# A two-layer hybrid encoder: the SSD gates as channel tiles among the heads, low parts of the odd weights by DMA

## The chip, the cores and the metric

The kernel runs on one core of a Trainium2 chip. The metric is the device time of one execution in microseconds; where several runs are shown, their median.

## The reference

The network has two layers on x of 512 positions and 1024 channels, and a final RMSNorm. The even layer (latent attention and a Conformer convolution) is not touched here. The odd layer, which the change is about, is:

```python
def odd_layer(x, norm_g, w_in, ...):
    u = rms_norm(x, norm_g) @ w_in                    # 1024 -> 1536 + 2560 + 48 + 4 x 512
    z_c, xbc, dt_f, dt_b, g_b, g_c, h_d, z_d = jnp.split(u, ...)
    o_c = ssd_mixer(z_c, xbc, dt_f, dt_b, ...)        # bidirectional Mamba-2
    o_d = short_conv(g_b, g_c, h_d, conv_d_w) * jax.nn.silu(z_d)
    return x + concatenate([o_c, o_d]) @ w_out        # 2048 -> 1024

def ssd_mixer(...):
    xbc = silu(dw_conv(xbc, conv_w) + conv_b)         # width 5, over positions
    xs, bm, cm = ...                                  # 24 heads of 64; B and C: 4 groups of 128
    y = ssd_scan(forward) + flip(ssd_scan(backward)) + d_skip * xs
    y = y * silu(z)                                   # the gate, 1536 channels
    return rms_norm(y in 4 groups of 384) * norm_g
```

`ssd_scan` works in 4 chunks of 128 positions: inside a chunk (C B^T, weighted by decays) times X; between chunks a state of 128 x 64 a head, carried with decays. All is float32.

## The kernel before

**Products in three parts.** Each float32 matmul operand is split into a high part (rounded to fp32r) and a low part (the rest), and a product is hi.hi + lo.hi + hi.lo: three fp32r matmuls. Activations are split once a layer (`xT`). Weights are split as they come, by the class `Weights`: `_prepare` takes the next slab of a list that has the order of use, loads it (an SP DMA) into `w_raw` (2 buffers), copies it with rounding to `w_hi` on ACT (line 87), and subtracts on DVE or POOL to get `w_lo` (line 88; 3 buffers each). For the odd layer's input projection the subtraction is POOL's. `next` hands out a slab and prepares up to `ahead + 1` = 2 slabs.

**Tiles of the odd layer's input projection.** `odd_tiles` lists the order. A *channel tile* (`mm_cm`, line 318) computes 128 channels x 512 positions in one PSUM bank `acc` (3 banks): 24 matmuls of 512 columns. A *token tile* product (`mm_tm`, line 345) has positions on the partitions. The gates z are made as token tiles, group by group (384 channels; in group 0 also the 48 raw dt columns): 4 position tiles, each 24 matmuls. They come first, all four groups of them, then the channel tiles: C, B and three x tiles of a group, and four short-convolution pieces (h, gc, gb, zd).

`channel_tile` also does what follows the product. For C, B and x: `conv5`, one ACT pass (line 718), four DVE taps that read PSUM (line 720), and a SiLU on ACT and DVE (lines 721 and 722). B and x are then transposed by PE into bank `sb` (line 266) and copied by ACT (lines 748 and 754), in the same call. `fill(n)` works off the next n entries of the list.

**SSD.** While group 1's gates run on PE, a chain on DVE, ACT and PE makes the step sizes dt and their running sums (lines 784 to 827). Then, for each of the 4 groups:

- `ssd_prepare`: C.B products (line 849), two masked copies, the chunk states (line 862 on PE, with DVE 860 and 868, POOL 867, ACT 865), one direction after the other.
- `ssd_pairs`, three pairs of heads: for each head the factor matrix f (ACT 898 and 903, DVE 899 and 904 in 128-column pieces, then Exp, line 906, and the product, line 907), its matmuls with x (line 910, bank `cv`), then the sums with the off-diagonal part (PE 926, DVE 919, 931, 934), the gate multiply on POOL (line 936), and `fill` with 1 to 3 channel tiles.
- `ssd_finish`: the group's RMSNorm (ACT 946, DVE 950) and 12 transposes back.

The decays e come from DRAM by an SP DMA that repeats a row over 128 partitions (line 879). At the end 13 output pages are split into high and low parts (lines 360 and 361), the last group's three by `split_psum`, and the output projection `oo` follows (line 345 again, 16 slabs).

**Order.** The code's order is the priority; the framework moves an instruction ahead within an engine's queue where its own estimate says it is ready. What stands in a queue then runs in order.

Of the kernel before, what the change touches and what calls it, by code (L numbers as in the profile page):

```python
# [69 lines left out]
class Weights:  # L70


    def __init__(self, tc, pool, slabs, ahead, raw_bufs, bufs):
# [4 lines left out]
    def _prepare(self):
# [8 lines left out]
        nc.scalar.copy(hi, raw)  # L87
        eng.tensor_tensor(lo, raw, hi.bitcast(F32), op=ALU.subtract)  # L88
# [71 lines left out]
def odd_tiles():  # L160
# [10 lines left out]
def trunk(ctx, tc, A, out, dbg=None):  # L171
# [560 lines left out]
    def channel_tile(kind, i):  # L732
        if kind == "z":
            n = GW if i else GW + NH
            for t, a in mm_tm("z", xT, 4, n, four(1 - i % 2)):
                if not i:
                    V.tensor_tensor(dtr[:, t], a[:, GW:GW + NH], prow("dt_bias"), op=ALU.add)
                gate(zg[i][:, t], a[:, :GW])
        elif kind == "C":
# [3 lines left out]
        elif kind == "B":  # L743
            bt = tmp("BT", "BT", 1)
            conv5("B", 12 + i, bt)
            tp = transposed([bt[:, t * P:(t + 1) * P] for t in range(NT)], "sb")
# [95 lines left out]
    def ssd_prepare(g):  # L842

        CT, BT, Bt, xs = (inp[g][k] for k in ("C", "B", "Bt", "x"))
        hs = heads(g)
# [9 lines left out]
        for d in range(2):  # L855
            seq = list(range(NT)) if d == 0 else list(range(NT - 1, -1, -1))
            prev = None
            for n, c in enumerate(seq[:-1]):
# [1 line left out]
                V.tensor_tensor(h3(w), h3(xs[:, c]), bc(dec[:, c, hs[d]], HPG, HD), op=ALU.mult)  # L860
# [1 line left out]
                T.matmul(sp[:, :GW], Bt[:, c * P:(c + 1) * P], w, start=True, stop=True)
                st = gw("St", 12)
                if prev is None:
                    SC.copy(st, sp[:, :GW])
                else:
# [1 line left out]
                    V.tensor_tensor(st, sp[:, :GW], st, op=ALU.add)
# [13 lines left out]
    def ssd_pairs(g, cbm, St, fills):  # L882
# [3 lines left out]
        for j in range(3):  # L886
            pr = slice(j * P, (j + 1) * P)
            yd = bank("cv")
            for i in range(2):
                hh = g * HPG + 2 * j + i  # L890
                hf, hb = hh, SH + hh

                decays(hh + 2)
                rb = ahead[hh]
                e, f = rb[:, 0], tmp("f", "f", 3)
                for c in range(NT):
                    cc = slice(c * P, (c + 1) * P)
                    SC.activation(f[:, cc], cbm[0][:, cc], AF.Copy, scale=dt[:, c, hf:hf + 1])  # L898
                    V.scalar_tensor_tensor(f[:, cc], cbm[1][:, cc], dt[:, c, hb:hb + 1], f[:, cc],  # L899
                                           op0=ALU.mult, op1=ALU.add)  # L900
                for c in range(NT):
                    cc = slice(c * P, (c + 1) * P)
                    SC.activation(e[:, cc], rb[:, 0, cc], AF.Identity, bias=nacs[:, c, hf:hf + 1])  # L903
                    V.scalar_tensor_tensor(e[:, cc], rb[:, 1, cc], nacs[:, c, hb:hb + 1], e[:, cc],  # L904
                                           op0=ALU.add, op1=ALU.min)
                SC.activation(e, e, AF.Exp)
                V.tensor_tensor(f, e, f, op=ALU.mult)
                for c in range(NT):
                    o = c * P + i * HD
                    T.matmul(yd[:, o:o + HD], f[:, c * P:(c + 1) * P],  # L910
                             xs[:, c, (2 * j + i) * HD:(2 * j + i + 1) * HD],
                             start=(i == 0 and c == 0), stop=(i == 1 and c == NT - 1), skip_group_check=True)

            yt = xs[:, :, pr]
            yd4 = yd.rearrange("p (c h d) -> p c h d", c=NT, h=2)
            y4 = yt.rearrange("p c (h d) -> p c h d", h=2)
            for i in range(2):
                hh = g * HPG + 2 * j + i
                V.scalar_tensor_tensor(y4[:, :, i], y4[:, :, i], dsk[:, hh:hh + 1], yd4[:, :, i],
                                       op0=ALU.mult, op1=ALU.add)  # L920
            for d in range(2):
                c0 = 1 - d
                yo = bank("tp")
                for n in range(3):
                    c = c0 + n
                    T.matmul(yo[:, n * P:(n + 1) * P], CT[:, c * P:(c + 1) * P], St[d][c][:, pr],  # L926
                             start=n == 0, stop=n == 2, skip_group_check=True)
                yw = gw("gt", 4)
                e2 = ea[:, c0:c0 + 3, hs[d].start + 2 * j:hs[d].start + 2 * j + 2]
                q4 = lambda a: a[:, :GW].rearrange("p (c h d) -> p c h d", c=3, h=2)  # L930
                V.tensor_tensor(q4(yw), q4(yo), e2.rearrange("p c (h o) -> p c h o", o=1).broadcast_to([P, 3, 2, HD]),
                                op=ALU.mult)
                yc = yt[:, c0:c0 + 3]
# [158 lines left out]
```

## Time and profile before

| | |
|---|---|
| median of 3 runs | 990.68 us (989.94 to 990.91) |
| the profiled execution | 989.05 us |
| its span | 987.2 us, granted PE clock 0.983 |
| busy: PE, DVE, ACT, POOL | 929.5, 737.1, 464.8, 385.2 us |
| gates of groups 1 to 3 on PE | 517.4 to 571.6 us |
| first channel tile to output projection | 571.6 to 891.1 us |

Times inside the profile are counted from the span's start. "Busy" leaves out instructions that only wait or issue. The ends of matmuls are modelled and overlap: the mean duration of one (some 0.4 us) is more than what it adds to a row of them.

### The profile page before, as it was taken

How to read it: one execution, taken by the hardware profiler on the slowest of the kernel's cores; microseconds unless marked ns; L12 is line 12 of the kernel's file. 1: busy time of each engine (PE TensorE's matmuls, PEld its weight loads, DVE VectorE, ACT ScalarE, POOL GpSimd, SP SyncE). 2: the span in 40 equal slices, each digit the busy share in tenths (PEclk: the TensorE clock that was granted, in tenths of full speed). 3: DMA queues.
4: the chain of work that ended last, by engine and by line, in shares of the span. 5: the costliest groups of instructions: out<-in, count | busy, mean ns of one | idle time of the engine just before them, and what ended most of it. 6: DMA issues, size and time to landing. Idle time of an engine off the chain costs nothing. (4 is left out here: it accounts for less than half of the span.)

```text
span 987.2 us, 12582 instructions
## 1 busy us (share of the span) xinstructions
PE 929.5 (94%) x4564; PEld 754.8 (76%) x4564; DVE 737.1 (75%) x1295; ACT 464.8 (47%) x916; POOL 385.2 (39%) x272
## 2 busy tenths in 40 slices
PE   7899999999999999999999999888878988999996
PEld 7887686686786777888899987766756876787885
DVE  4799888899898998952357457899898968956205
ACT  6646444454444544543242546455456555434312
POOL 0251734526337063461143454334423443445221
PEclk9999999999999999999999999999889999999999
DMA  8313312212212126233343533432332423322222
GB/s 307 102 30 112 56 54 66 70 25 102 70 25 96 52 69 168 71 112 107 123 142 89 172 110 104 106 86 86 107 107 88 124 89 103 111 101 90 87 86 86
DMA packets 42326, 95.99 MB, mean 97 GB/s; under 512 B 12136, under 2 KB 13800, under 8 KB 42264
## 3 DMA queue, kind: packets, MB, share of 16 engines
q1 hardware_dynamic: 42264, 95.19, 31.2%
q8 instruction: 36, 0.59, 0.2%
q14 instruction: 26, 0.21, 0.1%
HBM read 90.85 MB, written 4.33 MB: 96 GB/s over the span
## 5 line engine op out<-in xcount | busy, mean ns | idle before, releaser
L88 POOL TENSOR_TENSOR w_lo<-w_raw,w_hi 128x1024 fp32r<-128x1024 f32 (+2 forms) x68 | 160.4, 2361 | 254.2 <-ACT w_hi L87 155.1
L87 ACT CAST w_hi<-w_raw 128x1024 fp32r<-128x1024 f32 (+7 forms) x142 | 135.0, 952 | 202.9 <-PE acc L318 58.7
L318 PE MATMUL acc<-xT_hi,w_hi 128*128 128x512 f32 x544 | 223.1, 412 | 2.7 <-ACT xT_hi L406 2.7
L318 PE MATMUL acc<-xT_lo,w_hi 128*128 128x512 f32 x544 | 220.9, 407 | 0.0
L88 DVE TENSOR_TENSOR w_lo<-w_raw,w_hi 128x1024 fp32r<-128x1024 f32 (+6 forms) x74 | 83.8, 1132 | 96.8 <-ACT w_hi L87 92.5
L318 PE MATMUL acc<-xT_hi,w_lo 128*128 128x512 f32 x544 | 144.7, 400 | 0.0
L481 DVE SCALAR_TENSOR_TENSOR cv<-u,pc,cv 128x497 f32<-128x497 f32 (+10 forms) x176 | 130.2, 740 | 10.0 <-ACT cv L470 7.7
L318 PEld LDWEIGHTS acc<-xT_hi,w_hi 128*128 128x128 f32 x544 | 106.0, 195 | 25.6 <-ACT xT_hi L406 2.9
L318 PEld LDWEIGHTS acc<-xT_lo,w_hi 128*128 128x128 f32 x544 | 105.6, 194 | 22.4 <-POOL xT_lo L407 0.4
L318 PEld LDWEIGHTS acc<-xT_hi,w_lo 128*128 128x128 f32 x544 | 103.3, 192 | 21.3
L479 POOL TENSOR_TENSOR side<-side 128x510 f32<-128x510 f32 (+3 forms) x56 | 78.5, 1402 | 4.7
L484 POOL TENSOR_TENSOR u<-cs,side 128x512 f32<-128x512 f32 x8 | 11.0, 1374 | 157.1 <-issue 149.9
L533 ACT ACTIVATE p<-sb,mx 128x512 f32<-128x512 f32 x64 | 43.4, 684 | 20.9 <-DVE mx L531 20.6
L904 DVE SCALAR_TENSOR_TENSOR e<-e,nacs 128x128 f32<-128x128 f32 x96 | 45.9, 520 | 9.6 <-ACT e L903 9.6
L478 POOL TENSOR_SCALAR side<-u,pc 128x510 f32<-128x510 f32 (+3 forms) x56 | 50.2, 897 | 4.7
L899 DVE SCALAR_TENSOR_TENSOR f<-cbm,dt,f 128x128 f32<-128x128 f32 x96 | 47.4, 538 | 0.4 <-ACT f L898 0.4
L531 DVE TENSOR_REDUCE mx<-sb 128x1 f32<-128x512 f32 x64 | 41.7, 685 | 3.2 <-PE sb L529 2.4
L903 ACT ACTIVATE e<-e,nacs 128x128 f32<-128x128 f32 x96 | 31.4, 391 | 22.1 <-DMA e<-acs 18.9
L720 DVE SCALAR_TENSOR_TENSOR c<-acc,pc,c 128x510 f32<-128x510 f32 (+1 forms) x48 | 35.7, 743 | 7.7 <-ACT c L718 7.4
L266 PEld LDWEIGHTS tp<-kc,p 128*128 128x128 f32 x256 | 28.9, 140 | 16.0 <-ACT pt L556 10.7
L529 PE MATMUL sb<-k_t,qk_hi 128*128 128x512 f32 (+1 forms) x128 | 39.6, 404 | 0.5 <-DVE k_t L257 0.4
L566 PE MATMUL acc<-pt,v_tm 128*64 128x512 f32 x128 | 37.6, 608 | 1.5 <-DVE pt L556 1.5
(336 smaller groups left out, 1918.5 us busy)
## 6 DMA issues: line engine op xcount, KB each, us to landing
w_raw<-in_w_cm_o SPq DMA_DIRECT2D x36, 512.0 KB, 3.5
w_raw<-in_w_cm_e SPq DMA_DIRECT2D x32, 512.0 KB, 3.6
e<-acs SPq DMA_DIRECT2D x24, 512.0 KB, 5.2
w_raw<-in_w_out_e SPq DMA_DIRECT2D x16, 512.0 KB, 3.5
w_raw<-in_w_out_o SPq DMA_DIRECT2D x16, 512.0 KB, 3.5
w_raw<-in_w_z SPq DMA_DIRECT2D x12, 384.0 KB, 3.2
xt<-in_xT SPq DMA_DIRECT2D x8, 256.0 KB, 5.2
x_t<-in_x SPq DMA_DIRECT2D x4, 512.0 KB, 6.9
```

The source lines that it names most:

```text
L87: nc.scalar.copy(hi, raw)
L88: eng.tensor_tensor(lo, raw, hi.bitcast(F32), op=ALU.subtract)
L318: T.matmul(a, l, r, start=n == 0, stop=n == 3 * kk - 1)
L478: G.tensor_scalar(t[:, o], ut[:, i], wt(j), 0.0, op0=ALU.mult, op1=ALU.add)
L479: G.tensor_tensor(side[:, o], side[:, o], t[:, o], op=ALU.add)
L481: V.scalar_tensor_tensor(c[:, o], ut[:, i], wt(j), c[:, o], op0=ALU.mult, op1=ALU.add)
L529: T.matmul(s, l[:, qs], r, start=n == 0, stop=n == 2)
L531: V.tensor_reduce(mx, s, axis=AX.X, op=ALU.max, negate=True)
L533: SC.activation(p, s, AF.Exp, bias=mx, accum_out=sums[:, q:q + 1])
L566: T.matmul(o[j * HD:(j + 1) * HD], v_tm[:, k, (h0 + j) * HD:(h0 + j + 1) * HD], pt, start=k == 0, stop=k == NT - 1, skip_group_check=True)
L899: V.scalar_tensor_tensor(f[:, cc], cbm[1][:, cc], dt[:, c, hb:hb + 1], f[:, cc], op0=ALU.mult, op1=ALU.add)
L904: V.scalar_tensor_tensor(e[:, cc], rb[:, 1, cc], nacs[:, c, hb:hb + 1], e[:, cc], op0=ALU.add, op1=ALU.min)
```

## The change

1. **Gates.** Group 0's gate stays a token tile. The gates of groups 1 to 3 become nine channel tiles `zc` (3 a group), made as the others are, gated in channel layout (ACT and DVE) and transposed by PE into `zg`. They stand in the list between the groups' other tiles.
2. **Low parts by DMA.** For all channel tiles of the odd layer (`BY_DMA`, 45 slabs) ACT writes the rounded negative into `w_lo`, and a DMA issued by POOL adds `w_raw` to it in place. `next` prepares 4 slabs ahead of use instead of 2; every fourth slab has a buffer pair of its own, so there are 4.
3. **Transposes late.** `turn_later` puts off a tile's transposes until after the next tile's product.
4. **SSD in other pieces.** `ssd_factors` makes a pair's two factors, then `fill(3)` runs three channel tiles, then `ssd_pair` uses the factors. `ssd_states` takes the two directions in turn. Between groups come the C.B products of the next, the norm of the last, one tile, the states, the transposes back.
5. **End.** All channel tiles are used up before the last pair. The first 13 output pages are split around it, and the last group's norm and transposes (`last_group`) stand within the output projection, ahead of its seventh slab.
6. Buffers: `c5` 5 instead of 3, `f` 4 instead of 3, `gt` 5 instead of 4.

```diff
+BY_DMA = ("C", "B", "x", "zc", "h", "gc", "gb", "zd")
...
-        hi = self.pool.tile([P, D], F32R, name="w_hi", tag="w_hi", bufs=self.bufs)[:, :kt * n]
-        lo = self.pool.tile([P, D], F32R, name="w_lo", tag="w_lo", bufs=self.bufs)[:, :kt * n]
+        more = key in BY_DMA and self.i % 4 == 0
+        hi, lo = ((self.more if more else self.pool).tile([P, D], F32R, name=nm, tag=nm, bufs=1 if more else self.bufs)
+                  [:, :kt * n] for nm in ("w_hi", "w_lo"))
         nc.scalar.copy(hi, raw)
-        eng.tensor_tensor(lo, raw, hi.bitcast(F32), op=ALU.subtract)
+        if key in BY_DMA:
+            nc.scalar.mul(lo, raw, -1.0)
+            nc.gpsimd.dma_start(lo, raw, accum_op=ALU.add)
+        else:
+            eng.tensor_tensor(lo, raw, hi.bitcast(F32), op=ALU.subtract)
...
-        self.fetch(self.ahead + 1)
+        self.fetch(self.ahead + (3 if key in BY_DMA else 1))
...
-    return z + group(0) + group(1) + short(0) + group(2) + short(1) + group(3) + short(2) + short(3)
+    gates = lambda a, b: [("zc", i) for i in range(a, b)]
+    return ([("z", 0)] + group(0) + gates(3, 4) + group(1) + gates(4, 6) + short(0) + group(2) + gates(6, 9) + short(1)
+            + group(3) + gates(9, 12) + short(2) + short(3))
...
+        elif kind == "zc":
+            c = tmp("c5", "c5", 5)
+            gate(c, mm_cm("zc", xT))
+            turn_later(c, lambda tp: SC.copy(zg[i // 3][:, :, i % 3 * P:(i % 3 + 1) * P], c4(tp)))
...
+    def turn_later(c, put):
+        turns.append(lambda: put(transposed([c[:, t * P:(t + 1) * P] for t in range(NT)], "sb")))
 
     def fill(n):
         for _ in range(n):
-            kind_i = next(todo, None)
-            if kind_i:
-                channel_tile(*kind_i)
+            before = list(turns)
+            turns.clear()
+            channel_tile(*next(todo))
+            for t in before:
+                t()
...
-    fill(7)
-    pre = ssd_prepare(0)
-    for g in range(GRP):
-        ssd_pairs(g, *pre, ((2, 2, 1), (3, 3, 3), (3, 3, 3), (3, 3, 2))[g])
-        if g < GRP - 1:
-            pre = ssd_prepare(g + 1)
-        ssd_finish(g)
+    fill(5)
+    cbm, first = ssd_products(0)
+    St = ssd_states(0, first)
+    for g in range(GRP):
+        for j in range(3):
+            fs = ssd_factors(g, j, cbm)
+            fill(3)
+            if g == GRP - 1 and j == 2:
+                for i in range(KT // 2):
+                    split_page(i)
+            ssd_pair(g, j, fs, St)
+        if g < GRP - 1:
+            cbm, first = ssd_products(g + 1)
+            ssd_norm(g)
+            fill(1)
+            St = ssd_states(g + 1, first)
+            ssd_turn(g)
...
-        for t, a in mm_tm("oo", (oh, ol), 8, 512, four(h), 3 if h else 1):
+        for t, a in mm_tm("oo", (oh, ol), 8, 512, four(h), 3 if h else 1, None if h else (6, last_group)):
```

How it stands in the queues, at three places. PE while dt is made: `tp<-kc,d` turns the decays (d1), `tp<-kc,cs` turns their running sums back; before, among the gates of groups 1 and 2 (line 345):

```order
L345 MATMUL cv<-w_lo,xT_hi 128x384 x2
L266 MATMUL tp<-kc,d_4966 24x128 x4
L345 MATMUL sb<-w_hi,xT_hi 128x384
L345 MATMUL sb<-w_hi,xT_lo 128x384
L345 MATMUL sb<-w_hi,xT_hi 128x384
L813 MATMUL tp<-kc,cs 128x24
L345 MATMUL sb<-w_hi,xT_lo 128x384
L813 MATMUL tp<-kc,cs 128x24
```
```order
L323 MATMUL acc<-xT_lo,w_hi 128x512
L271 MATMUL tp<-kc,d_4891 24x128 x4
L323 MATMUL acc<-xT_hi,w_hi 128x512
L323 MATMUL acc<-xT_lo,w_hi 128x512
L323 MATMUL acc<-xT_hi,w_hi 128x512
L323 MATMUL acc<-xT_lo,w_hi 128x512
L830 MATMUL tp<-kc,cs 128x24
L323 MATMUL acc<-xT_hi,w_hi 128x512
L830 MATMUL tp<-kc,cs 128x24
```

Between group 0's gate and the first of these rows stood the 96 matmuls of group 1's gate; now stand 50 of the tiles C, B and x (line 323 is `mm_cm`).

PE at a pair of heads in group 0: `cv<-xs,f` are a head's four matmuls with its factors, `sb<-kc,BT` the transposes of B of the next group, `tp<-St,CT` the off-diagonal part. Before and now:

```order
L318 MATMUL acc<-xT_hi,w_lo 128x512 x5
L910 MATMUL cv<-xs,f 128x64 x4
L318 MATMUL acc<-xT_hi,w_lo 128x512
L266 MATMUL sb<-kc,BT 128x128 x4
L318 MATMUL acc<-xT_hi,w_lo 128x512 x2
L318 MATMUL acc<-xT_hi,w_hi 128x512
L318 MATMUL acc<-xT_lo,w_hi 128x512
L318 MATMUL acc<-xT_hi,w_hi 128x512
L318 MATMUL acc<-xT_lo,w_hi 128x512
L910 MATMUL cv<-xs,f 128x64 x4
```
```order
L323 MATMUL acc<-xT_lo,w_hi 128x512
L323 MATMUL acc<-xT_hi,w_lo 128x512 x8
L942 MATMUL cv<-xs,f 128x64 x8
L958 MATMUL tp<-St,CT 128x128
L271 MATMUL sb<-kc,BT 128x128 x4
L958 MATMUL tp<-St,CT 128x128 x5
L323 MATMUL acc<-xT_hi,w_hi 128x512
```

The two heads' matmuls have moved together behind whole tiles, and the transposes of B with them.

POOL from the first group on: `w_lo<-w_raw,w_hi` is the low part, `St` the chunk states, `xs<-xs,zg` the gate multiply. Before and now:

```order
L88 TENSOR_TENSOR w_lo<-w_raw,w_hi 128x1024 x9
L867 TENSOR_TENSOR St<-St,dtr 128x384 x4
L88 TENSOR_TENSOR w_lo<-w_raw,w_hi 128x1024
L936 TENSOR_TENSOR xs<-xs,zg 128x4x128
L88 TENSOR_TENSOR w_lo<-w_raw,w_hi 128x1024
L936 TENSOR_TENSOR xs<-xs,zg 128x4x128
```
```order
L92 DMA w_lo<-w_raw 128x1024 x10
L894 TENSOR_TENSOR St<-St,dtr 128x384 x4
L92 DMA w_lo<-w_raw 128x1024 x3
L968 TENSOR_TENSOR xs<-xs,zg 128x4x128
L92 DMA w_lo<-w_raw 128x1024 x3
L968 TENSOR_TENSOR xs<-xs,zg 128x4x128
```

A queue of subtractions has become one of DMA issues, three of them between two gate multiplies.

More of the change, by code (lines that the diff above doesn't have):

```diff
@@ L687, in trunk @@
     npage = {"keep": 4}
+    W.more = pg
     def bc(col, n, w):
@@ L840, in heads, with ssd_products @@
         return [slice(d * SH + g * HPG, d * SH + (g + 1) * HPG) for d in range(2)]
[L842 to L845 removed]
+    def ssd_products(g):
+        CT, BT = inp[g]["C"], inp[g]["B"]
         cb = bank("tp")
@@ L880, in decays, with ssd_factors @@
             ahead.append(e)
-    def ssd_pairs(g, cbm, St, fills):
+    def ssd_factors(g, j, cbm):
+        fs = []
+        for i in range(2):
+            hh = g * HPG + 2 * j + i
+            hf, hb = hh, SH + hh
+            decays(hh + 2)
+            rb = ahead[hh]
+            e, f = rb[:, 0], tmp("f", "f", 4)
+            for c in range(NT):
+                cc = slice(c * P, (c + 1) * P)
+                SC.activation(f[:, cc], cbm[0][:, cc], AF.Copy, scale=dt[:, c, hf:hf + 1])
+                V.scalar_tensor_tensor(f[:, cc], cbm[1][:, cc], dt[:, c, hb:hb + 1], f[:, cc],
+                                       op0=ALU.mult, op1=ALU.add)
+            for c in range(NT):
+                cc = slice(c * P, (c + 1) * P)
+                SC.activation(e[:, cc], rb[:, 0, cc], AF.Identity, bias=nacs[:, c, hf:hf + 1])
+                V.scalar_tensor_tensor(e[:, cc], rb[:, 1, cc], nacs[:, c, hb:hb + 1], e[:, cc],
+                                       op0=ALU.add, op1=ALU.min)
+            SC.activation(e, e, AF.Exp)
+            V.tensor_tensor(f, e, f, op=ALU.mult)
+            fs.append(f)
+        return fs
@@ L884, in ssd_pairs, with ssd_pair @@
+    def ssd_pair(g, j, fs, St):
         CT, xs = inp[g]["C"], inp[g]["x"]
         hs = heads(g)
[L886 to L933, printed above, removed]
-                V.tensor_tensor(yc, yc, yw.rearrange("p (c d) -> p c d", c=3), op=ALU.add)
-            zj = zg[g][:, :, pr]
-            G.tensor_tensor(yt, yt, zj, op=ALU.mult)
-            fill(fills[j])
@@ L939, in ssd_finish @@
-    def ssd_finish(g):
+        pr = slice(j * P, (j + 1) * P)
+        yd = bank("cv")
+        for i, f in enumerate(fs):
+            for c in range(NT):
+                o = c * P + i * HD
+                T.matmul(yd[:, o:o + HD], f[:, c * P:(c + 1) * P],
+                         xs[:, c, (2 * j + i) * HD:(2 * j + i + 1) * HD],
+                         start=(i == 0 and c == 0), stop=(i == 1 and c == NT - 1), skip_group_check=True)
+        yt = xs[:, :, pr]
+        yd4 = yd.rearrange("p (c h d) -> p c h d", c=NT, h=2)
@@ L982, in more, with split_page, last_group @@
         return free.pop(0)
-    oh, ol = split_pages(oF[:13], more, (big("o_hi"), big("o_lo")))
-    oh, ol = oh + [h for h, _ in last], ol + [l for _, l in last]
+    def split_page(n):
+        if not pair:
+            pair.extend((big("o_hi"), big("o_lo")))
+        hi, lo = (b[:, n] for b in pair) if n < KT else (more(), more())
+        SC.copy(hi, oF[n])
+        (V if n % 3 else G).tensor_tensor(lo, oF[n], hi.bitcast(F32), op=ALU.subtract)
+        op[0].append(hi)
+        op[1].append(lo)
+    fill(5)
[15 more added lines that the diff above has]
+            ssd_turn(g)
+    for i in range(KT // 2, 13):
+        split_page(i)
+    oh, ol = op
+    def last_group():
+        ssd_norm(GRP - 1)
+        ssd_turn(GRP - 1)
+        oh.extend(h for h, _ in last)
+        ol.extend(l for _, l in last)
     x1 = []
```

96 lines of the change are left out of this document (61 added, 35 removed).

## The prediction

> **What bounds the kernel now.** I read the page's busy shares first, then the chain that ended last, then a table of stretches, and inside the long stretch the groups and the waits. Rows of the page, and busy time by stretch (PE, PEld, DVE, ACT, POOL, then granted clock, DMA share, GB/s):
>
> ```profile
> span 987.2 us, 12582 instructions
> PE 929.5 (94%) x4564; PEld 754.8 (76%) x4564; DVE 737.1 (75%) x1295; ACT 464.8 (47%) x916; POOL 385.2 (39%) x272
> ```
> ```profile
> 0.00:517.40 517.40, 500.57 (x2481) 399.65 (x2482) 408.44 (x670) 248.01 (x470) 206.92 (x178) 1.00 0.31 93
> 517.40:571.60 54.20, 54.20 (x309) 51.86 (x308) 29.86 (x61) 23.95 (x49) 23.44 (x12) 1.00 0.43 131
> 571.60:891.10 319.50, 286.35 (x1391) 231.10 (x1390) 262.98 (x500) 165.57 (x358) 125.33 (x67) 0.96 0.33 101
> 891.10:987.20 96.10, 88.37 (x389) 72.18 (x387) 35.84 (x67) 27.27 (x42) 29.55 (x15) 0.98 0.25 88
> ```
>
> PE is the bound nearly everywhere, but the third row (from the first channel tile to the first matmul of the output projection) is different: PE stands still for 33.2 of 319.5 us and its clock is 0.96, while DVE is at 82%. The second row (the gates of groups 1 to 3 as token tiles) is the reverse: PE 100%, DVE 55%. So there is work on PE with nothing for DVE beside it, and then work for DVE that PE waits on. What a piece of PE work costs when PE is fed is read from the chain that ended last (start, us):
>
> ```profile
> 845.14 1.09 PE tp L266 x8
> ...
> 856.18 1.39 PE tp L926 x12
> 857.57 16.38 PE acc L318 x72
> 873.95 1.75 PE cv L910 x16
> ...
> 889.78 1.33 PE tp L266 x8
> ```
>
> A projection matmul advances by 16.38/72 = 0.2275 us (5.46 us a tile of 24), a pair's diagonal product takes 1.75, its off-diagonal one 1.39, four transposes 0.55. The counts for the stretch (busy, mean ns, idle before):
>
> ```profile
> 571.60:891.10 319.50, 225.03 (x864) 0.96 0.33 101
> ```
> ```profile
> L910 PE MATMUL cv<-xs,f 128*128 128x64 f32 x192 | 25.5, 281 | 9.1 <-DVE f L907 9.1
> L862 PE MATMUL tp<-gt,Bt 128*128 128x384 f32 x48 | 19.5, 516 | 2.8 <-DVE St L868 1.5 <-DVE gt L860 1.1
> L926 PE MATMUL tp<-St,CT 128*128 128x128 f32 x144 | 18.7, 277 | 0.0
> ```
>
> (The first row is line 318 alone.) PE's fed work there: 864 x 0.2275 = 196.6; 12 x 1.75 = 21.0; 12 x 1.39 = 16.7; states 19.5; 112 transposes (64 after convolutions, 48 at the groups' ends) in fours, 28 x 0.55 = 15.4; 32 products C.B at 0.136, 4.4. Sum 273.6 of 319.5 us. The missing 45.9 us are the 33.2 of standstill and 12.7 of slow running, which is what a clock of 0.96 takes from 319.5 us (12.8).
>
> What PE waits for there, and what slows DVE (first two rows are waits: total, times, longest; the rest is order of time, and one group):
>
> ```profile
> PEld cv L910 <- DVE f L907: 11.6, 7, 3.0
> PE sb L266 <- DVE c L722: 9.0, 4, 3.2
> ```
> ```profile
> 628.50 0.34 DVE L899 SCALAR_TENSOR_TENSOR f<-cbm,dt,f 128x128 f32<-128x128 f32 x1
> ...
> 640.99 3.90 DVE L899 SCALAR_TENSOR_TENSOR f<-cbm,dt,f 128x128 f32<-128x128 f32 x4
> ...
> 642.28 2.46 POOL L88 TENSOR_TENSOR w_lo<-w_raw,w_hi 128x1024 fp32r<-128x1024 f32 x1 [0.44 <-ACT w_hi L87]
> ```
> ```profile
> L88 POOL TENSOR_TENSOR w_lo<-w_raw,w_hi 128x1024 fp32r<-128x1024 f32 x35 | 87.6, 2504 | 119.3 <-PE acc L318 31.8 <-issue 27.1 <-ACT w_hi L87 20.2
> ```
>
> A head pair's factors and the convolution ahead of a transpose are what PE waits for. Four factor steps of 0.34 us took 3.90 where a low-part subtraction ran on POOL: 3.90 - 4 x 0.34 = 2.54, the whole POOL instruction. The Trainium skill (SBUF — State Buffer, "Who interferes with whom") says that a VectorE instruction with two SBUF inputs contends with a GpSimd one that reads SBUF, and that the second to come blocks fully; these rows agree.
>
> **The change, part by part.** *Gates of groups 1 to 3.* Removed: 288 matmuls of 384 columns, the second stretch's 54.2 us less its 21 other instructions (transposes and the like, an estimate of 2.9 us at 0.136), so 51.3. Added: 9 channel tiles, 9 x 5.46 = 49.1, and 36 transposes, 9 x 0.55 = 5.0. PE's work rises by 2.8 us. The gates' ACT and DVE steps work on as many columns as before (12 x 384 = 9 x 512), and the SP queue loads as many bytes in 9 pieces as in 12. PE's fed work from 517.4 to the output projection is then 273.6 + 2.9 + 49.1 + 5.0 = 330.6 us, where before it took 54.2 + 319.5 = 373.7. The floor of the change is thus 43.1 us, if PE never waits.
>
> *Factors ahead of three tiles.* A pair's PE slot is now 16.38 + 1.75 + 1.39 and up to three transposings, 1.65: 21.2 us. DVE and ACT rows for it:
>
> ```profile
> L720 DVE SCALAR_TENSOR_TENSOR c<-acc,pc,c 128x510 f32<-128x510 f32 (+1 forms) x48 | 35.7, 743 | 7.7 <-ACT c L718 7.4
> L907 DVE TENSOR_TENSOR f<-e,f 128x512 f32<-128x512 f32 x24 | 19.4, 809 | 3.1 <-ACT e L906 3.1
> L934 DVE TENSOR_TENSOR xs<-xs,gt 128x384 f32<-128x384 f32 x24 | 15.9, 665 | 0.0
> L931 DVE TENSOR_TENSOR gt<-tp,d 128x384 f32<-128x384 f32 x24 | 12.8, 546 | 0.0
> L919 DVE SCALAR_TENSOR_TENSOR xs<-xs,dsk,cv 128x256 f32<-128x256 f32 x24 | 10.6, 473 | 4.5 <-PE cv L910 4.4
> L722 DVE SCALAR_TENSOR_TENSOR c<-c5t,c 128x512 f32<-128x512 f32 x12 | 8.3, 689 | 6.5 <-ACT c5t L721 6.3
> ```
> ```profile
> L87 ACT CAST w_hi<-w_raw 128x1024 fp32r<-128x1024 f32 x36 | 37.5, 1042 | 29.7 <-PE acc L318 19.2 <-issue 6.2 <-DMA w_raw<-in_w_out_o 3.1
> L718 ACT ACTIVATE c<-acc,pc 128x512 f32<-128x512 f32 x12 | 9.3, 773 | 2.2 <-PE acc L318 2.2
> L721 ACT ACTIVATE c5t<-c 128x512 f32<-128x512 f32 x12 | 7.5, 626 | 6.8 <-DVE c L720 6.8
> ```
>
> ```profile
> L899 DVE SCALAR_TENSOR_TENSOR f<-cbm,dt,f 128x128 f32<-128x128 f32 x96 | 47.4, 538 | 0.4 <-ACT f L898 0.4
> L904 DVE SCALAR_TENSOR_TENSOR e<-e,nacs 128x128 f32<-128x128 f32 x80 | 38.1, 517 | 3.1 <-ACT e L903 3.1
> ```
>
> A convolved tile costs DVE 4 x 0.743 + 0.689 = 3.66 us, two heads' factors 16 x 0.34 + 2 x 0.809 = 7.1, a pair's rest 2 x (0.473 + 0.546 + 0.665) = 3.4. A slot of three convolved tiles is 21.5 us for DVE against 21.2 for PE; one of three gates or short pieces about 13. Over the two stretches together DVE has less to do than PE: 29.9 + 263.0, less the blocking. In the two groups above that is 96 x (0.538 - 0.34) + 80 x (0.517 - 0.34) = 33 us, and POOL keeps 125.3 - 87.6 = 37.7 of its 125.3 us, 0.3 of it, so 23 go. That leaves 270 us under 330.6. Where PE stops is then decided slot by slot. Three slots hold three convolved tiles (the first of group 0, the second of groups 1 and 2). They have no slack, and engines that run in order don't meet without any; I put 2 us on each (an estimate, between nothing and the 3.0 us that one wait for a factor cost at most): 6 us.
>
> *Transposes one tile late.* PE has 5.46 us of the next tile to cover 0.773 + 4 x 0.743 + 0.626 + 0.689 = 5.06 of ACT and DVE work. That is just enough where DVE does nothing between; a factor step or two between (0.34 each) overshoots by under 0.7. I count it with the 6 us.
>
> *Start.* The step sizes (dt) were worked out under the gate matmuls:
>
> ```profile
> 517.97 0.36 DVE L784 SCALAR_TENSOR_TENSOR d<-dtr 128x192 f32<-128x192 f32 x1
> ...
> 529.88 0.36 DVE L798 SCALAR_TENSOR_TENSOR d<-dt,aexp 128x192 f32<-128x192 f32 x1
> ...
> 543.57 0.36 DVE L827 TENSOR_TENSOR d<-d,dt 128x192 f32<-128x192 f32 x1 [0.43 <-ACT d L823]
> ```
>
> Now their cover is the C and B tiles. 50 matmuls (11.4 us) stand ahead of the first transposing of dt, which comes 12.3 us after the gate, plus four taps of C on DVE between, 3.0: a wait of 3.9. The interleaved single matmuls behind it (rows of PE in the section on the change) cover less than each scan and tap they wait for, about 4 more. So 8 us.
>
> *End.* Before, the last group's norm was covered by the last two tiles; now by six slabs of the output projection, 144 matmuls, ample. PE then needs ACT's cast of a weight slab (1.04) and the split of the last pages (0.7 each on ACT and DVE) before slab six: 2 us.
>
> *Low parts by DMA.* POOL loses the 35 subtractions, ACT gains 45 negated copies at 1.04 (as line 87) and 9 more casts: 165.6 + 24.0 + 56 = 246 us under 347, hidden by PE's matmuls (with that cover gone it would be 56 us more). Each low part now waits for cast, copy and an accumulating transfer, and holds the raw page until that has landed; there are two raw pages. POOL's queue is in order: a transfer behind a gating multiply (line 936) waits for the pair ahead, and covers it with the same three tiles. On the SP queue the 24 loads of decays stand between weight loads that now wait for an accumulate; a late one delays a factor that is needed three tiles on. No row shows an accumulating transfer. The nearest are
>
> ```profile
> w_raw<-in_w_cm_o SPq DMA_DIRECT2D x36, 512.0 KB, 3.5
> ...
> e<-acs SPq DMA_DIRECT2D x24, 512.0 KB, 5.2
> ```
>
> From below 3.5 us (a plain 512 KB load); from above 10.4 (two of the slower kind, since two pages are read). I take 5.2, nearer to one move of that size. A raw page is then held for 3.5 + 1.04 + 1.04 + 5.2 and some 1.4 of ACT's queue (lines 718 and 721), 7.0 + 5.2 = 12.2 us for two tiles, 6.1 a tile. PE takes 21.2/3 = 7.1. The supply holds, with three tiles in hand, up to a transfer of 7.1 us. The Trainium skill (DMA: Bandwidth & Descriptors, "Anatomy of one DMA — SWDGE (gpsimd) path") gives 2.0 us plus bytes over 436 GB/s, an estimate of 3.2 us here; by it the supply would be 5.1 us a tile and the sum the same.
>
> **Sum.** 330.6 + 6 + 8 + 2 = 346.6 against 373.7: 27.1 less, span 960.1. The profiled execution took 989.05 us, 1.85 over its span; the median of the runs shown, 990.68, lies 1.6 above it. 990.7 - 27.1 = 963.6, so 964. In this the 12.7 us of slow clock go with the standstills; if the 16 us of waits left bring it along in proportion (16/33.2 x 12.7 = 6), it is 970.
>
> **Rivals.** *PE never waits* (0.12): 990.7 - 43.1 = 947.6. For it: DVE's 270 us fit under 330. Against: the three heavy slots and the start.
>
> *The raw pages are the bound* (0.15). Place: the SP queue, whose load waits for the accumulate's landing. It decides from a transfer of 7.1 us on; at 9.6, (7.0 + 9.6)/2 x 45 = 373.5 us, the gain is gone; at 10.4, 391.5, it is 990.7 + 17.8 = 1008. For it: the transfers add at least 45 x 0.52 = 23.6 MB to a stretch that moves 101 GB/s at a share of 0.33. Against: even twice that keeps the share near 0.8.
>
> *Waits stay in proportion* (0.08): PE worked 273.6/319.5 = 0.856 of its stretch; 330.6/0.856 = 386, so 990.7 + 12.5 = 1003. For it: DVE and ACT run in order and the same pairs of engines wait for each other. Against: at both places where PE waited it now has a tile or three ahead.
>
> *The transfer's issue starves* (0.03): POOL cannot issue while DVE holds what both use. Behind one of the longest common DVE steps, 0.809 us (line 907), the transfer would count 6.0, still under 7.1, and cost nothing; behind three in a row, 2.4 us, it counts 7.6, (7.0 + 7.6)/2 = 7.3 a tile against 7.07, 45 x 0.23 = 10 us of the gain, 974. Against: on most of its steps here DVE is blocked by POOL, not the reverse. The Trainium skill (SBUF — State Buffer, "SBUF: two separate sides") warns that VectorE in a two-port mode locks GpSimd out of writing descriptors, and gives 620 ns against 3100 for a transfer; an estimate from those two figures adds 2.5 us, and the time would be 977. No run here shows it.
>
> **Numbers.** The forecast itself has 0.62, 953 to 977. The range 946 to 990 takes in the floor, the starved issue and the milder half of the raw pages. Under 0.2% (2 us) a measurement of this kernel tells nothing from no change. Faster: 0.62 + 0.12 + 0.03 + 0.06 = 0.83; same 0.03 (raw pages near 9.6); slower 0.06 + 0.08 = 0.14.
>
> **What would show it.** In the new profile PE's busy time from the first gate's end to the output projection should be near 335 of 347 with a clock of 0.99; line 921 should average under 0.42 us; w_lo by DMA should land in 4 to 7 us; PE's waits on factors should be gone and those on transposes stand in the heavy slots. Wrong would be: loads that wait for raw pages and PE waiting for w_lo, or PE's clock still at 0.96.

## The result and the profile after

The changed kernel took 994.46 us (median of 5 runs, 993.88 to 995.26); the kernel before, beside it on the same chip, 989.94. The ratio is 1.0054, 95% interval 1.0035 to 1.0074: half a per cent slower, where the forecast was 27 us faster. The profiled execution took 995.21 us, its span is 993.4.

First the top of the page, then the busy time by stretch (columns as before: PE, PEld, DVE, ACT, POOL, granted clock, DMA share, GB/s). The middle row runs from the end of group 0's gate to the first matmul of the output projection:

```profile
span 993.4 us, 12611 instructions
PE 935.8 (94%) x4528; PEld 754.4 (76%) x4528; DVE 694.3 (70%) x1292; ACT 505.8 (51%) x964; POOL 308.4 (31%) x269
```
```profile
0.00:517.10 517.10, 501.25 (x2480) 400.45 (x2481) 407.70 (x669) 249.51 (x470) 205.21 (x178) 1.00 0.31 94
517.10:895.70 378.60, 344.85 (x1654) 280.86 (x1653) 246.81 (x537) 227.03 (x444) 73.43 (x75) 0.93 0.67 165
895.70:993.40 97.70, 89.73 (x398) 73.08 (x397) 39.84 (x87) 29.29 (x50) 29.73 (x16) 0.97 0.24 86
```

The first row is as before; the last is 1.6 us longer than the 96.1 of before. All else is in the middle one: 378.6 us where the prediction had 344.6 (330.6 + 6 + 8) and before there were 373.7. DVE has become free (247 us of 379) and PE still stands for 33.7 us, at a lower clock than before: 0.93. What PE, then ACT, then the SP queue waited for there (total, times, longest):

```profile
PE sb L271 <- DVE BT L728: 14.1, 3, 6.8
PE sb L271 <- DVE c L728: 7.8, 3, 3.9
PE tp L271 <- DVE d L815: 4.3, 1, 4.3
...
PE tp L830 <- DVE cs L827: 1.3, 1, 1.3
```
```profile
ACT w_hi L89 <- DMA w_raw<-in_w_cm_o: 42.0, 15, 6.2
ACT e L925 <- DMA e<-acs: 21.9, 9, 6.8
```
```profile
SPq L85 <- DMA w_lo<-w_raw: 275.4, 44, 12.0
```

PE's waits on factors are gone. It now stands at transposes (21.9 us at bank `sb`) and while dt is made (5.6). ACT stands for weight pages and decays, and the SP queue, which loads both, stands 275 of 379 us for accumulating transfers to land. One of PE's waits, the longest, in the chain of waits (start, us):

```profile
773.94 1.19 issue
775.13 4.84 DMA w_lo<-w_raw
...
780.01 0.33 SPq L85
...
780.44 6.20 DMA e<-acs
...
787.03 0.97 ACT e L925 x3
...
788.84 0.62 ACT c5t L727
...
789.78 3.16 DMA w_raw<-in_w_cm_o
...
793.02 1.04 ACT w_hi L89
...
794.15 0.64 ACT c5t L727
...
794.81 0.70 DVE BT L728
...
795.56 1.12 PE sb L271 x4
```

Read upwards: PE waits to transpose B, whose SiLU waits for ACT. ACT works in order, and there two things stood ahead of it: the cast of a weight page whose load had started only at 789.78, and decays whose load had started only at 780.44. The decays stand behind a weight load in SP's queue (780.01), and that load waited for the transfer that landed at 779.97. So a raw page (a buffer `w_raw`) that comes free late reaches PE by way of ACT, not through a missing `w_lo`.

The profile page's rows of transfers (KB each, median us from issue to landing):

```profile
w_raw<-in_w_cm_o SPq DMA_DIRECT2D x45, 512.0 KB, 3.5
w_lo<-w_raw POOLq DMA_DIRECT2D x45, 512.0 KB, 5.3
e<-acs SPq DMA_DIRECT2D x24, 512.0 KB, 5.9
```

The transfer takes what the prediction took for it (5.2). But followed page by page through the trace (means of the 45: load's issue to landing 3.9, landing to cast 3.1, cast to the end of the negated copy 3.4, to the DMA's issue 0.5, issue to landing 5.8) a raw page is held for 16.7 us, and the next load goes out 0.06 us later. Two pages give a tile every 8.35 us; 45 x 8.35 = 376 of the 378.6 us. That sum alone shows only that the pages were never idle: it comes out near the stretch in any kernel that reloads a page as soon as it is free. Whether they are the bound has to be shown by changing their number.

Of the 6.5 us between landing and the end of the copy, the cast and the copy themselves are 2.1. For 2.7 (1.8 ahead of the cast, 0.9 between cast and copy) ACT was busy with other steps, and for 1.6 it stood. So the page waits more for ACT's own work than for what ACT itself waits for.

### The profile page after: what moved, and what is told of

It is laid out like the page before. It is cut to its first block, busy times and chain, and to the rows that moved or that the text cites. A ratio compares the mean times of both kernels' runs of the same rounds, so it can differ in the third digit from the quotient of the medians.

```text
span 993.4 us, 12611 instructions
## 1 busy us (share of the span) xinstructions
PE 935.8 (94%) x4528; PEld 754.4 (76%) x4528; DVE 694.3 (70%) x1292; ACT 505.8 (51%) x964; POOL 308.4 (31%) x269
## 4 chain that ended last, share of the span: by engine, by line
PE 66%; DVE 12%; DMA 11%; ACT 6%; issue 3%; POOL 0%; SPq 0%; DVEq 0%; ACTq 0%; POOLq 0%
PE acc L323 29%; PE acc L350 9%; PE tp L350 5%; PE sb L350 5%; PE sb L534 5%; DMA e<-acs 4%; PE tp L271 4%; DMA w_raw<-in_w_cm_o 3%; PE cv L350 3%; PE acc L571 3%; PE tp L958 2%; ACT w_hi L89 2%; DMA w_lo<-w_raw 1%; DMA w_raw<-in_w_cm_e 1%; PE cv L942 1%
## 5 line engine op out<-in xcount | busy, mean ns | idle before, releaser
L323 PE MATMUL acc<-xT_hi,w_hi 128*128 128x512 f32 x616 | 253.3, 412 | 2.7 <-ACT xT_hi L411 2.7
L323 PE MATMUL acc<-xT_lo,w_hi 128*128 128x512 f32 x616 | 250.0, 407 | 0.2 <-POOL xT_lo L412 0.2
L323 PE MATMUL acc<-xT_hi,w_lo 128*128 128x512 f32 x616 | 157.2, 394 | 0.0
L323 PEld LDWEIGHTS acc<-xT_hi,w_hi 128*128 128x128 f32 x616 | 119.6, 194 | 28.0 <-ACT xT_hi L411 2.9
L323 PEld LDWEIGHTS acc<-xT_lo,w_hi 128*128 128x128 f32 x616 | 119.4, 194 | 25.1 <-POOL xT_lo L412 0.8
L323 PEld LDWEIGHTS acc<-xT_hi,w_lo 128*128 128x128 f32 x616 | 116.5, 190 | 24.2
L92 POOL DMA_DIRECT2D w_lo<-w_raw x45 | 39.3, 873 | 226.4 <-ACT w_lo L91 138.5
L94 POOL TENSOR_TENSOR w_lo<-w_raw,w_hi 128x1024 fp32r<-128x1024 f32 (+1 forms) x20 | 48.1, 2406 | 111.7 <-ACT w_hi L89 111.7
L91 ACT ACTIVATE w_lo<-w_raw 128x1024 fp32r<-128x1024 f32 x45 | 47.6, 1057 | 0.6 <-PE acc L323 0.6
L926 DVE SCALAR_TENSOR_TENSOR e<-e,nacs 128x128 f32<-128x128 f32 x96 | 33.4, 386 | 18.1 <-ACT e L925 18.1
L925 ACT ACTIVATE e<-e,nacs 128x128 f32<-128x128 f32 x96 | 32.3, 393 | 21.9 <-DMA e<-acs 21.9
```

What stands on the lines that cost most here:

```text
L91: nc.scalar.mul(lo, raw, -1.0)
L323: T.matmul(a, l, r, start=n == 0, stop=n == 3 * kk - 1)
```

## The experiments

Theory 1: the two raw pages bound the stretch. Rivals: A, the order on ACT (later: the new order as a whole); B, the 16 DMA engines, busy 0.67 of the stretch, or transfers that slow each other; and the decays' place in SP's queue. Ratios are to the kernel before, which took 995 to 997 us on the chips of e1 to e16 and 989.94 on that of the changed kernel, which was not run again beside them. "Stretch" is the middle row above, "standing" is PE's idle time in it.

| run | ratio (95%) | stretch, us | standing | clock |
|---|---|---|---|---|
| before (its own profile) | 1 | 373.8 | 33.1 | 0.96 |
| changed kernel (its own profile) | 1.005 (1.004 to 1.007) | 378.6 | 33.7 | 0.93 |
| e1 low part from HBM | 0.994 (0.992 to 0.997) | 372.4 | 27.4 | 0.96 |
| e2 no accumulate | 0.975 (0.969 to 0.980) | 354.6 | 14.5 | 0.99 |
| e3 low part by POOL | 1.023 (1.018 to 1.029) | 402.1 | 46.8 | 0.93 |
| e4 before + low part by DMA | 0.987 (0.983 to 0.992) | 365.6 | 26.9 | 0.98 |
| e5 four raw pages | 0.986 (0.980 to 0.991) | 365.4 | 25.6 | 0.98 |
| e6 three pairs | 1.009 (1.006 to 1.011) | 381.0 | 36.8 | 0.96 |
| e7 casts on POOL | 1.034 (1.030 to 1.038) | 414.0 | 62.2 | 0.92 |
| e8 decays on POOL | 1.013 (1.009 to 1.017) | 390.5 | 43.9 | 0.94 |
| e9 four pages, decays on ACT | 0.960 (0.956 to 0.963) | 342.3 | 7.0 | 1.00 |
| e10 decays on ACT alone | 1.009 (1.006 to 1.012) | 390.1 | 40.3 | 0.95 |
| e11 before + DMA + four pages + decays on ACT | 0.957 (0.954 to 0.960) | 336.6 | 4.7 | 1.00 |
| e12 e9, a third by POOL | 0.974 (0.970 to 0.977) | 353.1 | 15.5 | 0.99 |
| e13 three pages, decays on ACT | 0.964 (0.960 to 0.967) | 345.0 | 8.6 | 1.00 |
| e14 e1 + decays on ACT | 0.972 (0.968 to 0.977) | 349.9 | 13.7 | 1.00 |
| e15 before + decays on ACT | 0.998 (0.995 to 1.001) | 376.0 | 32.1 | 0.97 |
| e16 before + DMA + four pages | 0.982 (0.978 to 0.985) | 360.6 | 21.6 | 0.98 |

**e1: the page free before the transfer.**

```diff
-            nc.gpsimd.dma_start(lo, raw, accum_op=ALU.add)
+            nc.gpsimd.dma_start(lo, ap, accum_op=ALU.add)
```

> The accumulating transfer reads the weight from HBM again instead of the raw page, so a raw page is free after cast and negated copy. Theory (raw pages bound the stretch): in the changed kernel a page was held 16.7 us on average (load 3.9, wait for the cast 3.1, cast to end of copy 3.4, issue 0.5, transfer 5.8), two pages, 8.35 us a tile, 45 tiles = 376 of the stretch's 378.6 us. Without issue and transfer the hold is 10.4, 5.2 us a tile, less than PE's 7.07: the stretch falls to PE's pace, about 335 to 350 us, and the time to 950 to 968. Rival A (ACT's queue in order is the bound and the pages' hold only follows it): the waits inside ACT stay and the time stays within 985 to 995. Rival B (the 16 DMA engines, busy 0.67 of the stretch, are the bound): the same bytes are moved, the time stays at 990 to 998.

It gained about 1% on the changed kernel, far less than theory 1 had said (950 to 968 us; it took 989.74). Plain loads were slow beside these transfers:

```profile
w_raw<-in_w_cm_o SPq DMA_DIRECT2D x45, 512.0 KB, 5.2
w_lo<-in_w_cm_o POOLq DMA_DIRECT2D x45, 512.0 KB, 8.0
w_raw<-in_w_cm_e SPq DMA_DIRECT2D x32, 512.0 KB, 3.5
e<-acs SPq DMA_DIRECT2D x24, 512.0 KB, 6.9
```

The third row, of the even layer, shows what a load takes without accumulates beside it; in e2, where they are left out, the first row has 3.5 too. That an accumulate takes 8.0 here and 5.3 in the changed kernel can be the traffic or the source in HBM; no run separates them. ACT still stood 26.2 us for decays. This run alone spoke for B or A.

**e2: no accumulate.** The DMA's line is left out, and with it the part of the product that needs the low part.

> The accumulating transfers are left out (w_lo keeps the negated copy alone, so this part of the low parts isn't computed); the rest of the work is the same. Theory (raw pages): hold 10.4 us, 5.2 us a tile, time 948 to 966, near the first run of this call. Rival A (ACT's queue): 985 to 995. Rival B (DMA engines): 45 transfers of 512 KB less, time 960 to 975, clearly below the run that reads HBM.

0.975, the stretch 354.6: without the transfers the new order runs within 10 us of the 344.6 predicted. That speaks against A, but page and traffic are both gone here.

**e3: low parts by POOL again**, the rest as changed.

```diff
-        if key in BY_DMA:
-            nc.scalar.mul(lo, raw, -1.0)
-            nc.gpsimd.dma_start(lo, raw, accum_op=ALU.add)
-        else:
-            eng.tensor_tensor(lo, raw, hi.bitcast(F32), op=ALU.subtract)
+        eng.tensor_tensor(lo, raw, hi.bitcast(F32), op=ALU.subtract)
```

> Only the low parts by DMA are undone: POOL subtracts again for all channel tiles, with four slabs ahead and everything else as in the changed kernel. Theory (raw pages): hold = 3.9 + 3.1 + 1.04 + 2.5 and a wait in POOL's queue of 1 to 3, some 12 us, 6 us a tile, under PE's 7.07; DVE gets its blocking back (about 30 us, 280 of 340 us busy): 962 to 980. Rival A (the order on ACT, or the gates as channel tiles and the late transposes themselves, cost the time): 988 to 1000.

All expectations missed: 1.023, the stretch 402.1. The rest of the change without its second part is a clear loss. Rows of the stretch (DVE's two factor steps, then the longest wait of the SP queue):

```profile
L917 DVE SCALAR_TENSOR_TENSOR f<-cbm,dt,f 128x128 f32<-128x128 f32 x96 | 47.1, 529 | 0.5 <-ACT f L916 0.5
L922 DVE SCALAR_TENSOR_TENSOR e<-e,nacs 128x128 f32<-128x128 f32 x96 | 42.8, 483 | 10.7 <-ACT e L921 10.7
```
```profile
SPq L85 <- POOL w_lo L90: 263.8, 43, 15.4
```

The blocking is back, and the loads wait for POOL's queue as long as they had waited for transfers. Which of the two costs more wasn't separated.

**e4: the kernel before with low parts by DMA alone** (the same three lines added there).

> The kernel before with the low parts by DMA alone (two slabs ahead, no extra buffers). Theory (raw pages): 36 tiles at 8.35 us or more are 300 us of a stretch of 319.5, and each wait in that stretch that a late page causes comes on top, DVE's relief is 23 to 33 us off its 263: no gain, 986 to 1005. The reasoning of the prediction (transfers hidden, DVE relieved): 975 to 985.

0.987, as the prediction's reasoning had it. Its supply sum doesn't hold here either:

```profile
SPq L85 <- DMA w_lo<-w_raw: 228.2, 35, 11.7
```

Followed as above, a page is held for 16.3 us, not 12.2, and the next load goes out 0.07 us after it is free. But only 36 slabs pass through the two pages instead of 45, since the gates of groups 1 to 3 keep POOL's subtraction. That these nine slabs make the 1.8% between this kernel and the changed one would fit, but no run shows it.

**e5 and e6: four raw pages, and the control.** Two further pages lie in the room of the fourth pair; e6 has the last two edits alone.

```diff
-        raw = self.pool.tile([P, D], F32, name="w_raw", tag="w_raw", bufs=self.raw_bufs)[:, :kt * n]
+        own = key in BY_DMA and self.i % 2 == 0
+        raw = (self.more if own else self.pool).tile([P, D], F32, name="w_raw", tag="w_raw", bufs=self.raw_bufs)[:, :kt * n]
...
-        more = key in BY_DMA and self.i % 4 == 0
+        more = False
...
-        self.fetch(self.ahead + (3 if key in BY_DMA else 1))
+        self.fetch(self.ahead + (2 if key in BY_DMA else 1))
```

> Four raw pages instead of two, in the room of the fourth pair of high and low part (three pairs, three slabs ahead). In the changed kernel PE's 21.9 us of waits at transposes come where ACT, in order, stands for a raw page (42 us) or for decays (21.9) with the convolution's steps behind it. Theory 1 (pages): the hold of 16.7 us is now shared by four pages, 4.2 us a tile; loads land long before their casts, ACT's waits for w_raw fall below 10 us, the stretch to 350 to 360 us, ratio to the kernel before 0.965 to 0.985. Theory 2 (the transfers slow each other, as in the run that read HBM, where loads took 5.6 and accumulates 8.0 us): loads and accumulates overlap more, ratio 0.99 to 1.005.

> The control for the four raw pages: two raw pages, no fourth pair, three slabs ahead. Theory 1 (pages): with two raw pages the fourth pair is hardly used; as the changed kernel, ratio to before 1.00 to 1.01. If a fourth slab ahead only puts casts that must wait in front of the convolution's steps on ACT: 0.985 to 0.998. If the pairs carry it: above 1.012.

From 1.009 to 0.986: 2.3% for the pages. ACT no longer stands for a late weight load, but the stretch is 365.4, not 350 to 360. The chain of waits of e5 shows what is left:

```profile
536.36 7.66 DMA w_lo<-w_raw
...
544.07 0.35 SPq L86
...
544.47 3.22 DMA acs<-cs
...
547.74 6.58 DMA e<-acs
...
556.84 1.90 ACT e L926 x7
...
559.73 0.64 ACT c5t L728
560.37 0.02 issue
560.39 0.70 DVE c L729
561.09 0.04 issue
561.13 0.66 PE sb L272 x4
```

A weight load that nobody needs yet waits for its page; behind it in SP's queue waits the write of the running sums, and behind that the first decays, which ACT needs at once.

**e7: casts and copies on POOL.**

```diff
-        nc.scalar.copy(hi, raw)
         if key in BY_DMA:
-            nc.scalar.mul(lo, raw, -1.0)
+            nc.gpsimd.tensor_copy(hi, raw)
+            nc.gpsimd.tensor_scalar(lo, raw, -1.0, None, op0=ALU.mult)
```

> High part and negated copy are made by POOL instead of ACT, for the channel tiles; the order and the pages are the same. A one-input POOL step on 1024 columns should take about 1.8 us by the row of 0.913 us for 510. Theory 3 (ACT's queue: it is not the supply itself but ACT standing in order for a page, with the convolution's steps behind it, that stops PE): ACT waits no more, PE's waits at transposes fall from 21.9 to under 8 us, ratio 0.965 to 0.985. Theory 1 (pages alone): the hold is 3.9 + 2 x 1.8 + 0.9 + 5.8 and queueing, 14 to 16 us, 7 to 8 a tile against PE's 7.07: 0.99 to 1.005. If POOL's steps block DVE (3.6 us a tile, 45 tiles): above 1.005.

The test failed on its own cost: POOL's negated copy took 2.83 us, not 1.8, POOL was busy 250 of 414 us, and SP's loads waited 306 us for transfers, more than the 275 before. DVE's step at line 922 (921 in the changed kernel) rose from 406 to 505 ns, as in the third case of those expected, where POOL's steps block DVE. The run tells nothing of theory 3.

```profile
L91 POOL TENSOR_SCALAR w_lo<-w_raw 128x1024 fp32r<-128x1024 f32 x45 | 127.5, 2834 | 11.1 <-PE acc L324 10.9
L90 POOL CAST w_hi<-w_raw 128x1024 fp32r<-128x1024 f32 x44 | 52.3, 1189 | 100.9 <-PE acc L324 55.9 <-DMA w_raw<-in_w_cm_o 42.5 <-PE cv L943 2.1
```

**e8 and e10: decays on another queue, two pages.** The line `nc.sync.dma_start(e, ...)` becomes `nc.gpsimd.` (e8) or `nc.scalar.dma_start(e, ...)` (e10).

> The 24 loads of decays go to POOL's queue, so that they no longer stand between weight loads that wait for pages. If their lateness is what matters (ACT waits 21.9 us for them): those waits fall below 8, PE's waits at transposes halve, ratio 0.985 to 0.998. If they only wait elsewhere (behind accumulates and gate multiplies, in order): 1.00 to 1.015.

> The changed kernel with two raw pages and only the decays moved to ACT's queue. Theory 1 (pages first): SP's loads still wait for pages, ACT still stands 40 us for them: 0.998 to 1.008. If the decays alone carry it: 0.980 to 0.992.

No gain: 1.013 and 1.009. In e10 ACT waits only 1.3 us for decays, and stands 73.6 us for weight pages instead of 42.0:

```profile
ACT w_hi L89 <- DMA w_raw<-in_w_cm_o: 73.6, 19, 8.2
```

The pages come first.

**e9: both.** The edits of e5 and of e10.

> Four raw pages (as before in this study) and the 24 loads of decays issued by ACT instead of SP. With four pages the ratio was 0.986, PE still stood 18.6 us at transposes, and ACT stood 29.7 us for decays, whose loads wait in SP's queue behind weight loads that wait for pages. Theory 1b (the pages' wait reaches PE through the decays too): ACT's waits for decays fall below 10 us, PE's at transposes below 10, the stretch from 365 to 350 to 357, ratio 0.970 to 0.980. Rival (the decays are late because transfers of 512 KB slow each other, 5.2 to 6.2 us): 0.982 to 0.992.

0.960, beyond what was expected (956.85 us, the kernel before 997.11). The stretch, PE's largest wait, and SP's:

```profile
517.10:859.38 342.28, 335.23 (x1699) 274.97 (x1698) 248.74 (x543) 232.91 (x452) 77.55 (x79) 1.00 0.75 185
```
```profile
PE tp L890 <- DVE St L896: 4.0, 5, 1.2
```
```profile
SPq L86 <- DMA w_lo<-w_raw: 283.6, 42, 13.9
```

SP waits for the transfers as long as ever, but nothing urgent stands behind it. Waits at convolutions' transposes are gone (0.4 us are left), and the DMA share has risen to 0.75: B was not the bound. Together the four runs say that both were needed: with the decays on SP, four pages give 0.986 and two 1.009 (e5, e6); with the decays on ACT, 0.960 and 1.009 (e9, e10).

**e13 and e14: three pages; two pages, free before the transfer.** Both with decays on ACT; e13 has `% 3` for `% 2` and one page of its own, e14 is e1 with that line.

> As the four pages with decays on ACT (0.960), with three raw pages. Theory 1 by the prediction's own sum: hold 16.7 us (half of it queueing that shrinks) over three pages, 5.6 us a tile, under PE's 7.07: supply ample, ratio 0.957 to 0.968. If transfers slowing each other are the limit, the number of pages beyond two matters by how early loads go: 0.970 to 0.990.

> Two raw pages, each free after cast and copy (low parts accumulated from HBM), four pairs, decays on ACT. Theory 1 (hold) with the decays' queue as the second half: hold 10.4 us, 5.2 a tile, decays no longer behind it: 0.960 to 0.972. If the transfers' pace is the limit (8.0 us for an accumulate from HBM in the first run of this kind): 0.980 to 0.995.

Three pages do (0.964, stretch 345.0), as 16.7/3 = 5.6 us a tile against 7.07 says. For that sum the hold must be taken where pages are short: in e13 a page is held for 21.9 us and in e9 for 28.8, since a page that was loaded early lies full until its cast (13.7 us in e9, 3.1 in the changed kernel), and 21.9/3 = 7.3 and 28.8/4 = 7.2 then only follow the pace of the tiles. In e14 the page is free once it is copied, and two do nearly as well (0.972), although accumulates from HBM take 7.9 us there. So it is the hold over the number of pages, and most of what kept e1 from its gain was the decays' queue (0.994 to 0.972).

**e12: a third of the low parts by POOL** (`if key in BY_DMA and self.i % 3:` in e9).

> As the four pages with decays on ACT, with every third low part subtracted by POOL again: 15 transfers less, 15 POOL steps of 2.5 us more. If transfers slowing each other is what is left: 3 to 8 us better than the same without it. If POOL blocking DVE costs more: 3 to 10 us worse (15 x 2.5 = 37 us of POOL, of which about 0.6 falls on DVE work).

13 us worse, where 3 to 10 were expected for this case. Each of the 15 exchanges of a transfer for a subtraction costs 0.86 us of time.

**e15, e16, e11: the kernel before with the decays on ACT; with low parts by DMA and four pages (and three slabs ahead); with all three.**

> The kernel before with the decays' loads on ACT's queue alone; low parts stay subtractions. There SP's loads wait for POOL's subtraction, not for a transfer. If the decays' queue matters there too (PE waited 9 to 12 us for factors): 0.983 to 0.995. If not: 0.997 to 1.003.

> The kernel before with low parts by DMA and four raw pages, decays still on SP. Alone the low parts gave 0.987, with pages and decays 0.957. If the pages carry more of the rest: 0.960 to 0.970. If the decays do: 0.975 to 0.988.

> The kernel before with the low parts by DMA, four raw pages, three slabs ahead and the decays on ACT's queue: what supply and relief of DVE give without the new order, the gates as channel tiles and the late transposes. The kernel before with the low parts by DMA alone had 0.987, its stretch 311 of 319.5 us. If pages are what holds that one too: 0.970 to 0.980. If the order of the kernel before is what is left there (transposes right behind their tile): 0.983 to 0.990. Against the four-page version of the changed kernel it tells what the rest of the change is worth.

0.998, 0.982 and 0.957. The decays' place costs nothing measurable where loads wait for a subtraction, and 2.5% where they wait for a transfer and there are four pages (with two, in e10, moving them gained nothing). The last is the fastest of all (953.13 us, below the 0.970 to 0.980 expected), without the gates as channel tiles, the factors ahead or the late transposes:

```profile
517.10:853.75 336.65, 331.97 (x1727) 278.87 (x1727) 261.00 (x566) 222.52 (x445) 90.85 (x80) 1.00 0.70 174
```

PE stands for 4.7 us in it. Once weights and decays arrive, the new order has nothing left to win, and its 2.8 us of added PE work and 2.4 us more of standing make most of the 5.6 us between this stretch and that of e9.

## Why the prediction was wrong

**The step that failed** is "The supply holds" in the part on low parts by DMA. The hold was summed to 12.2 us, 6.1 a tile, from a load of 3.5, two ACT steps of 1.04, 1.4 of ACT's queue and the transfer. The transfer came out close (5.3 in the median, 5.8 in the mean), with some luck, since no row had shown one and the bounds were 3.5 and 10.4. What was short is ACT's part: 6.5 us from landing to the end of the copy instead of 3.5. The 1.4 us put down for ACT's queue were 2.7 of other steps and 1.6 of standing; the cast and the copy stand in order among these, and only in 11 of the 45 pages are they neighbours. With the load (3.9) and the issue (0.5) that made 16.7, 8.35 a tile, above PE's 7.07. The rival "the raw pages are the bound" was asked only for the length of the transfer; its turning point was already passed by the other terms. It had 0.15; with 10.9 measured in place of its 7.0 its formula gives (10.9 + 5.8)/2 x 45 = 376, no gain, as happened. That the pages were the bound is shown by e5, e9 and e13, which add pages.

**A second step failed with it:** "a late one delays a factor that is needed three tiles on". The decays behind waiting loads were priced at nothing. The factor has three tiles of time, but ACT has none: it stops at the first step on late decays, with the next tile's convolution behind. The Trainium skill (TensorE: Matmul & The Clock Gate, "Architectural detail: the array is 16× 32×32, not 1× 128×128") says that ACT and DVE are strict FIFO; the chain from 780 to 795 us agrees.

**Late transposes** were counted within 6 us; PE stood 21.9. ACT's and DVE's 5.06 us fit under 5.46 of cover only if ACT is free when the product ends. In e9, where late pages and decays no longer hold it up, 0.4 us is left of these waits.

**Factors ahead:** right. No wait on them is left, and the factor steps fell as said (line 921 under 0.42):

```profile
L921 DVE SCALAR_TENSOR_TENSOR f<-cbm,dt,f 128x128 f32<-128x128 f32 x96 | 35.2, 406 | 0.0
L926 DVE SCALAR_TENSOR_TENSOR e<-e,nacs 128x128 f32<-128x128 f32 x96 | 33.4, 386 | 18.1 <-ACT e L925 18.1
```

**Start and end:** 8 us foreseen for the start, 5.6 measured in the changed kernel and none in e9. For the end 2 us were foreseen, and the last row is 1.6 longer. That the two are close is luck: the foreseen wait isn't there, since the trace lists no wait of PE in that row, and some 1 us of the 1.6 is work that moved into it (12 transposes of the last group where 5 stood before, 7 x 0.136). The 6.2 us of standing that are left, in the states and the turning back of a group, were not foreseen; e9 still has 6.6 of them.

**Clock:** it was to come back with fewer standstills. As much standing stayed, in longer pieces, and it fell to 0.93. The stretch of 378.6 is 330.6 of fed work, 33.7 of standing and 14.3 left over. The clock stood at half for 54.6 us of the stretch, and PE was busy in 39.5 of them, so at half pace up to 19.7 us were lost (an estimate). I put most of the 14.3 down to the slow clock; no run separates it, and e9, whose clock is 1.00, has 4.7 left over too.

**PE's fed work:** 330.6 nearly holds. In e9 the stretch less its standing is 342.3 - 7.0 = 335.3, 4.7 more. The time forecast (a ratio of 0.973) was, if anything, too high for a kernel whose supply holds: e9 has 0.960.

## What to carry to other kernels

For a buffer that is held through a chain, sum the hold from the load's issue to the release with the queue of every engine on the way as it really stands, and compare hold over buffers with the consumer's pace; when an off-path step (here a transfer instead of a subtraction) is put into that chain, add a buffer in the same change. Loads that wait for buffers should not share a queue with loads that someone needs now. And when a change has several parts, price each alone: here one part (the transfer) with two buffers and a queue moved was worth 4% (e11); the rest added nothing to it (e9), and without it cost 2.3% (e3).

## What the runs showed of the hardware

- A 512 KB accumulating transfer within SBUF took 5.3 us in the median, 5.8 in the mean. Its issue held POOL for 0.87 us. The median was 5.1 in e4, at a DMA share of 0.67 among the channel tiles, and 5.8 and 6.2 in e9 and e13, at 0.75 in the stretch; from HBM it was 8.0 (e1). From the Trainium skill (DMA: Bandwidth & Descriptors, "Anatomy of one DMA — SWDGE (gpsimd) path") an estimate of 3.2 us follows for such a size. The measurement decides.
- The clock fell to half within each of the six standstills of 2.6 us or more in the changed kernel's stretch, 1.1 to 2.5 us after its start, and at none of the others, which were 1.3 us at most. In the kernel before it fell at two of 1.9 and 2.0 us and not at one of 2.4. Two rows of ten us each, one with a standstill of 2.6 us, one with pieces up to 1.15:

```profile
597.10:607.10 10.00, 7.39 (x43) 6.86 (x42) 8.15 (x18) 7.94 (x19) 1.21 (x2) 0.83 0.92 207
...
747.10:757.10 10.00, 8.55 (x40) 6.01 (x39) 10.00 (x28) 7.98 (x21) 3.07 (x4) 1.00 0.61 136
```

  The Trainium skill (TensorE: Matmul & The Clock Gate, "HAM oscillation — how this bites in real kernels") gives idle gaps over about 3.4 us as what to avoid. Here shorter ones were enough.
- POOL's one-input copy with a factor took 2.83 us for 1024 columns, its plain cast 1.19 (e7).
